# A hybrid decoder layer on one core: recurrent projections token-major, and every instruction issued from a recorded list

## The chip, the core and the metric

The kernel runs on one core of a Trainium2 chip. TensorE (PE) multiplies matrices into the accumulation memory (PSUM); VectorE (DVE), ScalarE (ACT) and GpSimd (POOL) work on arrays; SyncE (SP) issues transfers (DMAs) between the core's memory (SBUF) and the chip's main memory. Each engine executes its own instruction list in order and waits on semaphores where an instruction needs what another engine or a transfer makes. The metric is the device time of one execution in microseconds (us).

## The reference

One layer, 256 tokens, width 1024, float32:

```python
h = rmsnorm(x, norm1_g)
u = h @ w_in                       # columns: x_rnn | g_rnn | q | k | v | gates, 1024 each (gates 2048)
xa = causal_dwconv(x_rnn, conv_w, conv_b)                  # 4 taps over the tokens
ya = rg_lru(xa, w_r, b_r, w_i, b_i, lam) * gelu(g_rnn)     # block-diagonal gates, then a scan over tokens
yb = attention(rmsnorm(q), rmsnorm(k), v)                  # 8 heads of 128; one block of 256, so causal attention
merged = sigmoid(g_A) * (ya @ w_proj_rnn) + sigmoid(g_B) * (yb @ w_proj_attn)
x = x + merged @ w_out
h = rmsnorm(x, norm2_g)
x = x + (gelu(causal_dwconv(h @ w_up)) * (h @ w_gate)) @ w_down      # D_FF 2816
```

## The kernel before

**Products.** Each float32 operand is split into a rounded high part and a low remainder, and each product is three matmuls: high by high, low by high, high by low (lines 293 to 295, `mm3`). A product can be laid out in two ways. Feature-major (`fm_mm`, line 297): a 128x128 piece of the weight is held in the array and the 256 tokens stream past, so that the result has channels on the partitions; one matmul is 256 columns. Token-major (`tm_mm`, line 524): 128 tokens are held and 512 weight columns stream past, so that the result has tokens on the partitions; one matmul is 512 columns. In the kernel before, x_rnn (`rx`) and g_rnn (`rg`) are feature-major; k, q, v, the gates (`ga`, `gb`), both merge projections (`pr`, `pa`) and nearly all of up and gate (`up`, `gt`) are token-major.

**Units and chunks.** `UNITS` gives the order of PE's units: rx0 to rx3, rg0 to rg3, k0 to k3, ri0 (the block-diagonal r and i gates), q0, q1, ri1, ga, q, v and so on, then the merge, w_out, and the feed-forward part. Each unit consumes one chunk of weights, 1 MB. `load_next` (line 256) issues its DMA on SP into one of three `raw` buffers; `split_part` (line 274) makes `hi` on ACT (line 275; four buffers) and `lo` on DVE (line 276; three buffers). The table `AFTER` says at which quarter of which unit the other work is recorded, for instance "k1.3": "s11 conv2 decay" records the split of chunk 11, a convolution and the decay constants. Within that order, the scheduler of the tile framework places the instructions on ACT, DVE, POOL and SP; only the splits of the first stage are in written order on ACT and DVE (line 399).

**First stage.** Four chunks (rx) come in pieces of one, one, two, two and two k-tiles, each piece one DMA per chunk: rows of 1 KB for the first two pieces, then 2 KB, beside pieces of the transposed input `xT`. `xgh` and `xgl` are the input times norm1_g, split (lines 403 and 406). PE first runs `WARM` = 9 matmuls on a constant (line 342).

**Norm and layout.** The factor 1/rms of a token is computed while PE already multiplies (`norm1_stats`, line 416). For feature-major results it must lie along the free axis: `norm1_bcast` (line 425) spreads it with two matmuls, and DVE multiplies it in while it empties PSUM (line 470 for rx, line 724 for rg). For token-major results it is a scalar per partition, and ACT applies it.

**Turns.** q, k, up and gate are wanted feature-major and come out token-major. `turn` (line 314) turns them: DVE transposes 32x32 blocks (lines 321 and 323), four DMAs write the half (512 KB) to main memory, and a fifth, placed by its own item of `AFTER`, reads it back.

**Second norm.** `norm2_t` (line 785) transposes x on PE and makes the split input of the feed-forward part with four ACT and four DVE instructions of 128x128 in each of four calls (lines 794 and 795).

**Recurrence.** `rx_conv` (line 472) convolves along tokens, `ri_split` and `ri` make the gates, `lru_a` to `lru_d` the scan, `ya_mul` (line 660) multiplies by gelu(g_rnn).

Of the kernel before, what the change touches and what calls it, by code (L numbers as in the profile page):

```python
# [8 lines left out]
F32 = mybir.dt.float32  # L9
# [3 lines left out]
OP = mybir.AluOpType  # L13
# [17 lines left out]
HALVES, SMALLS, WARM, RAWS = 23, 10, 9, 3  # L31
# [6 lines left out]
    "rx0.0": "stats s4",  # L38
    "rg0.2": "bcast",
    "rg1.0": "evac3",  # L40
    "rg1.2": "s5",
    "rg1.3": "s6",
    "rg2.0": "evac0",
    "rg2.1": "evac2",
    "rg3.1": "evac1 conv0",
    "rg3.3": "s7",
    "k0.0": "s8 s9",
    "k1.0": "gelu1",
    "k1.1": "s10",
    "k1.3": "s11 conv2 decay",  # L50
    "k2.0": "krs0 s12 conv1 conv3",
    "k2.1": "split0 split1",
    "k2.2": "s13",
    "k2.3": "s14",
    "k3.2": "ks0",
    "ri0.0": "s15",
    "ri0.2": "krs1",
    "q1.3": "ks1 rk1",
    "ri1.2": "rk0",
    "ri1.3": "s16",  # L60
    "ga0.2": "rq0",
    "ga1.0": "qrs0",
    "ga1.2": "s17",
    "q2.0": "s18",
    "q3.0": "s19",
    "q3.2": "Tq0 Tk0",
    "v0.3": "s20",
    "v1.0": "Tk1",
    "v1.1": "la0",
    "v1.2": "S3 s21",  # L70
    "ga2.1": "rq1 S0 S1 Tq1 S2",
    "ga2.2": "s22 P3",
    "ga2.3": "s23",
    "ga3.0": "s24 s25 lb0 la1",
    "ga3.1": "lb1 lc1 ld1",
    "ga3.2": "P1",
    "v2.0": "s26",
    "v2.1": "qrs1 P0 P2",
    "v2.2": "gelu0 s27",
    "v2.3": "S4 s28",  # L80
    "v3.1": "S7",
    "v3.3": "S6",
    "gb0.0": "s29",
    "gb0.1": "lc0",
    "gb1.0": "S5",
    "gb1.1": "P4 s30",
    "gb1.2": "O3",
    "gb1.3": "O1",
    "gb2.0": "s31",
    "gb2.1": "O2",  # L90
    "gb2.3": "ld0",
    "gb3.0": "ya1 ya0",
    "gb3.1": "s32 P5 ys0",
    "gb3.2": "O4",
    "gb3.3": "sb0 s33",
    "pr0.1": "P7",
    "pr0.3": "s34 ys1",
    "pr1.1": "s35",
    "pr1.2": "sa1 sa0",
    "pr1.3": "O5 P6",  # L100
    "pr2.1": "s36",
    "pr2.3": "O7",
    "pr3.0": "O0",
    "pr3.1": "s37 O6",
    "pr3.3": "sb1",
    "pa2.2": "m0",
    "pa3.2": "s38",
    "pa3.3": "s39",
    "wo.1": "m1",
# [3 lines left out]
    "wo.12": "n00 s41",  # L113
    "wo.13": "n10",
    "up00.0": "s42 n01",
    "up00.2": "s43 n11",
    "gt00.3": "s44",
    "up01.1": "s45",
    "up01.3": "s46",
    "gt01.2": "s47",  # L120
    "up10.0": "ur0 s48",
    "up10.1": "s49",
    "up10.2": "bcast2",
    "up11.0": "s50",
    "up11.1": "s51",
    "up11.2": "fu0",
    "gt10.0": "s52",
    "gt10.1": "gr0",
    "up20.2": "s53",
    "up20.3": "ur1",  # L130
    "up21.0": "fg0",
    "up21.3": "s54 fu1",
    "gt20.2": "s55",
    "gt20.3": "gr1",
    "dn1.3": "s56 fg1",
    "up30.3": "s57 s58",
    "up31.0": "s59",
    "up31.2": "gr2",
    "up31.3": "s60 ur2",
    "gt31.0": "ur3",  # L140
    "gt31.1": "s61",
    "gt31.3": "fu2 s62",
    "dn2.0": "fu3 s63",
    "dn2.1": "fg2",
    "dn2.2": "s64",
    "dn3.0": "s65",
    "up40.0": "gr3",
    "gt40.0": "s66",
    "gt41.1": "s67",
    "gt41.2": "s68 fg3",  # L150
    "gt41.3": "ur4",
    "dn4.0": "s69",
    "dn4.1": "gr4",
    "dn5.1": "fu4",
    "dn5.2": "s70",
    "dn6.2": "s71",
    "dn7.0": "fg4",
    "last.3": "s72",
    "dn8.1": "s73",
    "dn9.3": "s74",  # L160
}


@with_exitstack
def trunk_layer(ctx: ExitStack, tc: tile.TileContext, xT, x, vec, win_fm, win_tm, wri, wpr, wpa,
                wout, wup, wgate, wdown, out):
    nc = tc.nc
    PSUM = bass.MemoryType.PSUM
    const = ctx.enter_context(tc.tile_pool(name="const", bufs=1))
    wp = ctx.enter_context(tc.tile_pool(name="wp", bufs=RAWS))  # L170
    halfp = ctx.enter_context(tc.tile_pool(name="halfp", bufs=HALVES))
    work = ctx.enter_context(tc.tile_pool(name="work", bufs=2))
    dram = ctx.enter_context(tc.tile_pool(name="dram", bufs=4, space=bass.MemoryType.DRAM))
    psA = ctx.enter_context(tc.tile_pool(name="psA", bufs=4, space=PSUM))
    psB = ctx.enter_context(tc.tile_pool(name="psB", bufs=4, space=PSUM))
# [30 lines left out]
    class Wide:  # L206


        def __init__(self, name, dt=F32):
            self.h = [half(f"{name}{i}", dt) for i in range(2)]  # L210

        def __getitem__(self, at):
            s = at[1]
            i = s.start // 1024
            assert (s.stop - 1) // 1024 == i
            return self.h[i][:, s.start - i * 1024:s.stop - i * 1024]

# [12 lines left out]
    source = {"rx": lambda c: win_fm[c], "rg": lambda c: win_fm[4 + c], "ri": lambda c: wri[c],  # L230
# [100 lines left out]
    tok32 = lambda a, t: a.rearrange("p (c t i b) -> p t c i b", t=2, i=4, b=32)[:, t]  # L331
# [3 lines left out]
    pv = const.tile([P, V_N], F32, name="pv")  # L335
    nc.scalar.dma_start(pv, vec)
# [8 lines left out]
    pieces = [(0, 1), (1, 2), (2, 4), (4, 6), (6, 8)]  # L345
    START = 4
    for i in range(START):
        if i < 2:
            raw[i] = wp.tile([P, 2048], F32, tag="raw", name=f"raw{i}")
            split_tiles()  # L350
        else:
            raw[i], hi[i], lo[i] = Wide(f"raw{i}"), Wide(f"hi{i}", F32R), Wide(f"lo{i}", F32R)
    ptr["load"] = ptr["split"] = START
    xs = const.tile([P, 2, D], F32, name="xs")
    for a, b in pieces:
        nc.sync.dma_start(kt(xTs.half(a // 4))[:, a % 4:a % 4 + b - a, :], xT[:, a:b, :])
        for i in range(START):
            s = slice(a * 256, b * 256)
            (nc.scalar if b <= 2 and i >= 2 else nc.sync).dma_start(raw[i][:, s], stream[i][:, s])
        if a == 0:  # L360
            nc.scalar.preload_act_table(AF.Exp)
        if a == 4:
            for t in range(2):
                nc.sync.dma_start(xs[:, t, :], x[t * P:(t + 1) * P, :])
# [3 lines left out]
    make_identity(nc, ident)  # L368
# [30 lines left out]
    with tc.manual_schedule(engines={mybir.EngineType.Activation, mybir.EngineType.DVE}):  # L399
        for a, b in pieces:  # L400
            for k in range(a, b):
                g = pv[:, V_G1 + k:V_G1 + k + 1]
                nc.scalar.activation(xgh[k], xTs[k], AF.Copy, scale=g)  # L403
                if a == 0:
                    split_part(0, slice(a * 256, b * 256), True)
                nc.vector.scalar_tensor_tensor(xgl[k], xTs[k], g, f(xgh[k]), op0=OP.mult, op1=OP.subtract)
            for i in range(a == 0, START):
                split_part(i, slice(a * 256, b * 256))

    rbc = const.tile([P, S], F32, name="rbc")  # L410
    rs1 = const.tile([P, 2], F32, name="rs1")
    dg = const.tile([P, 2, P], F32, name="dg")

    squared = []

    def norm1_stats():
        ss = const.tile([P, 2], F32, name="ss1")
        sq = half("sq1")
        for t in range(2):
            squared.append(nc.scalar.activation(sq, xs[:, t, :], AF.Square, accum_out=ss[:, t:t + 1]).ins)  # L420
        rsqrt(ss, rs1, 1.0 / D, 2)
        for t in range(2):
            nc.vector.tensor_scalar(dg[:, t, :], ident, rs1[:, t:t + 1], None, op0=OP.mult)

    def norm1_bcast():

        ps = bank("rbcp")
        for t in range(2):
            nc.tensor.matmul(ps[:, t * P:(t + 1) * P], ones, dg[:, t, :], start=True, stop=True)
        nc.scalar.copy(rbc, ps[:, :S])  # L430
# [4 lines left out]
    def make_decay():  # L435
# [9 lines left out]
        with tc.issue_after(squared[-1]):  # L445
            nc.scalar.activation(w[:, 1, :], w[:, 0, :], AF.Exp, scale=-1.0)
# [22 lines left out]
    def rx_evac(c, ps):  # L469
        nc.vector.tensor_mul(xr.pair(c), ps, rbc[:, None, :].to_broadcast([P, 2, S]))  # L470
# [66 lines left out]
    nc.vector.scalar_tensor_tensor(gqk, pv[:, V_QG:V_QG + 1], SC, pv[:, V_KG:V_KG + 1], op0=OP.mult, op1=OP.mult)  # L537
# [116 lines left out]
    rbc2 = rbc[:, None, :].to_broadcast([P, 2, S])  # L654
    open_ps, rx_ps = {}, {}
# [4 lines left out]
    def ya_mul(h):  # L660
        nc.vector.tensor_mul(gr.half(h), gr.half(h), it.half(h))

    def ya_split(h):
        split2(yah.half(h), yal.half(h), gr.half(h))
# [33 lines left out]
    evac = {"v": v_evac, "pr": pr_evac, "pa": pa_evac, "ga": lambda g, ps: gate_evac(sga, g, ps),  # L698
            "gb": lambda g, ps: gate_evac(sgb, g, ps)}

    def run_unit(kind, c):

        i = chunk[kind, c]
        if kind == "rx":

            for n in range(START):
                rx_ps[n] = kt(psA.tile([P, 512], F32, tag="A", name=f"rx{n}"))
            for k in range(KT):
                for n in range(START):
                    fm_mm(rx_ps[n], n, xgh, xgl, (k,), True)  # L710
            yield
            return
# [5 lines left out]
        elif kind == "rg":  # L718
            ps = fm_ps(f"{kind}{c}")
            for j in range(2):  # L720
                for h in range(2):
                    fm_mm(ps, i, xgh, xgl, range(4 * h, 4 * h + 4), js=(j,))
                    if j and h:
                        nc.vector.tensor_mul(gr.pair(c), ps, rbc2)
                    yield
        else:
            g, kh = c // 2, c % 2
            if not kh:
                open_ps[kind] = [bank(f"pa{g}{t}") if kind == "pa" else
                                 psA.tile([P, 512], F32, tag="A", name=f"{kind}{g}{t}") for t in range(2)]  # L730
# [9 lines left out]
    for n in range(4):  # L740
        item[f"evac{n}"] = lambda n=n: rx_evac(n, rx_ps[n])
        item[f"conv{n}"] = lambda n=n: rx_conv(n)
# [293 lines left out]
```

## Time and profile before

| | |
|---|---|
| time, median of 3 runs | 440.4 us (440.0 to 441.07) |
| profiled execution, its own time | 440.18 us |
| span of the profiled execution | 438.4 us |
| PE busy | 431.3 us, 98% |
| DVE busy | 325.1 us, 74% |
| ACT busy | 248.5 us, 57% |
| POOL busy | 45.8 us, 10% |
| moved by DMA | 95.89 MB, mean 219 GB/s |

The span runs from the first to the last instruction of the profiled execution. A busy share is an average over stages. Matmuls are pipelined: the duration of one matmul in the profile is longer than the distance from its start to the start of the next, so what a stream of matmuls costs is read from starts. PE's records count an operation on plain float32 operands (warm-up, transposes) twice.

### The profile page before, as it was taken

The numbers are of one execution on the slowest core, as the hardware profiler recorded it, in microseconds if no ns is written. First come the engines' busy times: TensorE is split into PE (matmuls) and PEld (weight loads), VectorE is DVE, ScalarE is ACT, GpSimd is POOL, SyncE is SP. The second block draws the span as 40 slices with busy tenths as digits, with TensorE's granted clock in tenths as the row PEclk, the third lists the DMA queues.
The fourth block names the chain that finished last, engine by engine and source line by source line (L and its number), as shares of the span: only waits on it lengthen the run. The fifth ranks groups of instructions, "written<-read, shape, count | busy, mean of one in ns | idle before, by whom it ended". The sixth has DMA issues, their size and how long they took to land.

```text
span 438.4 us, 5841 instructions
## 1 busy us (share of the span) xinstructions
PE 431.3 (98%) x2224; PEld 368.4 (84%) x2224; DVE 325.1 (74%) x448; ACT 248.5 (57%) x294; POOL 45.8 (10%) x99
## 2 busy tenths in 40 slices
PE   8999999999899999999999999999999999999996
PEld 8999988887788888888888888888888888888985
DVE  4689869768789999765576796576776779965943
ACT  4596748682888999944232373345437257352910
POOL 2038306424240000000000000000000000000000
PEclk9999999999999999999999999999999999999999
DMA  7987652857877754554553555877995494897202
GB/s 218 387 310 256 229 193 62 240 227 233 301 253 238 230 184 151 183 171 171 191 193 96 193 191 155 280 284 275 321 309 187 148 395 190 293 340 288 86 1 96
DMA packets 30268, 95.89 MB, mean 219 GB/s; under 512 B 2848, under 2 KB 12448, under 8 KB 26144
## 3 DMA queue, kind: packets, MB, share of 16 engines
q1 hardware_dynamic: 29520, 94.91, 62.0%
q10 hardware_dynamic: 720, 0.61, 0.6%
q8 instruction: 17, 0.28, 0.3%
q14 instruction: 11, 0.09, 0.1%
HBM read 87.12 MB, written 8.39 MB: 218 GB/s over the span
## 4 chain that ended last, share of the span: by engine, by line
PE 87%; DVE 5%; POOL 3%; DMA 2%; issue 1%; ACT 1%; SPq 0%; DVEq 0%
PE acc L293 4%; PE acc L294 4%; PE acc L295 4%; PE up L293 4%; PE up L294 4%; PE gt L293 4%; PE gt L294 4%; PE up L295 4%; PE gt L295 4%; POOL rsq L388 2%; DMA raw<-in_win_fm 2%; PE rg L295 2%; PE rg L294 2%; PE rg L293 2%; PE gb L293 2%; PE v L294 2%
## 5 line engine op out<-in xcount | busy, mean ns | idle before, releaser
L276 DVE TENSOR_TENSOR lo<-raw,hi 128x2048 fp32r<-128x2048 f32 (+3 forms) x92 | 170.9, 1868 | 40.1 <-ACT hi L275 8.5
L275 ACT CAST hi<-raw 128x2048 fp32r<-128x2048 f32 (+3 forms) x88 | 137.6, 1576 | 90.7 <-PE pa L295 16.0
L294 PE MATMUL up<-lo,h2h 128*128 128x512 f32 x80 | 31.2, 391 | 0.0
L294 PE MATMUL gt<-lo,h2h 128*128 128x512 f32 x80 | 31.1, 389 | 0.0
L294 PE MATMUL acc<-lo,fah 128*128 128x512 f32 x80 | 31.1, 389 | 0.0
L293 PE MATMUL acc<-hi,fah 128*128 128x512 f32 x80 | 31.1, 389 | 0.0
L295 PE MATMUL up<-hi,h2l 128*128 128x512 f32 x80 | 31.0, 389 | 0.0
L295 PE MATMUL gt<-hi,h2l 128*128 128x512 f32 x80 | 31.0, 389 | 0.0
L293 PE MATMUL up<-hi,h2h 128*128 128x512 f32 x80 | 30.9, 392 | 0.0
L293 PE MATMUL gt<-hi,h2h 128*128 128x512 f32 x80 | 30.8, 389 | 0.0
L295 PE MATMUL acc<-hi,fal 128*128 128x512 f32 x80 | 30.5, 389 | 0.0
L853 ACT ACTIVATE fc<-fu,pv 128x256 f32<-128x256 f32 x20 | 10.4, 590 | 19.8 <-DVE fu L865 19.8
L293 PE MATMUL rx<-xgh,hi 128*128 128x256 f32 x64 | 18.3, 288 | 0.8 <-ACT xgh L403 0.8
L295 PE MATMUL rx<-xgh,lo 128*128 128x256 f32 x64 | 18.2, 284 | 0.2 <-DVE lo L276 0.2
L293 PE MATMUL rg<-xgh,hi 128*128 128x256 f32 x64 | 18.2, 284 | 0.0
L294 PE MATMUL rx<-xgl,hi 128*128 128x256 f32 x64 | 18.2, 284 | 0.0
L295 PE MATMUL rg<-xgh,lo 128*128 128x256 f32 x64 | 18.1, 283 | 0.0
L294 PE MATMUL rg<-xgl,hi 128*128 128x256 f32 x64 | 18.1, 283 | 0.0
L293 PEld LDWEIGHTS up<-hi,h2h 128*128 128x128 f32 x80 | 15.0, 188 | 3.3 <-ACT h2h L794 0.2
L293 PEld LDWEIGHTS gt<-hi,h2h 128*128 128x128 f32 x80 | 15.0, 188 | 3.2
L295 PEld LDWEIGHTS gt<-hi,h2l 128*128 128x128 f32 x80 | 15.0, 188 | 3.2
L295 PEld LDWEIGHTS acc<-hi,fal 128*128 128x128 f32 x80 | 15.0, 188 | 3.1
(251 smaller groups left out, 1078.5 us busy)
## 6 DMA issues: line engine op xcount, KB each, us to landing
raw<-in_win_tm SPq DMA_DIRECT2D x12, 1024.0 KB, 5.2
raw<-in_win_fm SPq DMA_DIRECT2D x11, 1024.0 KB, 5.7
raw<-in_wup SPq DMA_DIRECT2D x11, 1024.0 KB, 5.7
raw<-in_wgate SPq DMA_DIRECT2D x11, 1024.0 KB, 5.7
raw<-in_wdown SPq DMA_DIRECT2D x11, 1024.0 KB, 6.0
raw<-in_wpr SPq DMA_DIRECT2D x4, 1024.0 KB, 5.0
raw<-in_wpa SPq DMA_DIRECT2D x4, 1024.0 KB, 4.9
raw<-in_wout SPq DMA_DIRECT2D x4, 1024.0 KB, 4.8
```

Of the source, the lines that this page charges most:

```text
L275: (nc.vector.tensor_copy if on_dve else nc.scalar.copy)(hi[i][:, s], raw[i][:, s])
L276: nc.vector.tensor_sub(lo[i][:, s], raw[i][:, s], f(hi[i][:, s]))
L293: nc.tensor.matmul(o, ah, bh, start=start, stop=False, skip_group_check=skip)
L294: nc.tensor.matmul(o, ah, bl, start=False, stop=False, skip_group_check=skip)
L295: nc.tensor.matmul(o, al, bh, start=False, stop=stop, skip_group_check=skip)
L388: nc.gpsimd.tensor_tensor(z, y, y, op=OP.mult)
L853: nc.scalar.activation(c, u, AF.Identity, scale=w(2), bias=pv[:, V_FB + m:V_FB + m + 1])
```

## The change

1. `rx` and `rg` become token-major. `run_unit` multiplies rx with 128 tokens held and 512 columns streaming, k-tile by k-tile, into four PSUM tiles of the `psA` pool; rg takes the general token-major path with four banks of `psB`. `norm1_bcast`, its two matmuls and the copy after them are gone.
2. The results are emptied by ACT with the token's factor as scalar (`scaled`: four copies of 128x512 for rx, four for rg) and turned with `turn`, two halves each: per half one transpose of 128x1024 on DVE, four DMAs out, one back. For x, ACT then reorders the blocks with two copies per half (`rx_order`). For g_rnn, gelu works on the blocks as they come back and `ya_mul` reads them in block order, two instructions per half instead of one; the product is written to `it`.
3. The first stage is cut otherwise: four pieces of two k-tiles; each DMA takes two chunks with rows of 2 KB; only the first is cut in two. The norm weights come in a small DMA of their own (`g1`); all other vectors come after the rx chunks, and x after two further chunks. `WARM` is 11.
4. `norm2_t` makes the split input with one multiplication, one copy and one subtraction over all four k-tiles.
5. All operations are recorded (`Later`), PE's in one list and the others in another, and issued in the order of the list `ORDER` under a manual schedule for all engines. `Pool` gives a recorded tile its buffer when it is issued: the one whose last use lies furthest back. `AFTER` is new in most entries.
6. Two small POOL instructions replace the DVE instruction that makes `gqk`.

By the built instruction lists, PE goes from 2211 to 2031 matmuls: `rx` from 192 of 256 columns to 84 of 512 and 24 of 256, `rg` from 192 of 256 to 96 of 512, minus two for the spread, plus two for the warm-up. ACT loads its function tables 14 times instead of 11. SP issues 185 DMAs instead of 173 and ACT 1 instead of 5: 20 new ones for the four turns, fewer in the first stage.

```diff
-HALVES, SMALLS, WARM, RAWS = 23, 10, 9, 3
+HALVES, SMALLS, WARM, RAWS = 23, 10, 11, 3
...
+class Later:
...
+    def issue(self, order):
...
+        for self.now, (engine, name, a, k) in enumerate(ops):
+            getattr(engine, name)(*map(real, a), **{n: real(v) for n, v in k.items()})
...
+    load_x(0, 2)
+    load_w(0, 0, one)
+    nc.scalar.preload_act_table(AF.Exp)
+    load_w(0, 0, two_)
+    load_w(0, 1)
+    for a in range(1, 4):
+        load_x(2 * a, 2 * a + 2)
+        for c in range(2):
+            load_w(a, c)
...
-    def rx_evac(c, ps):
-        nc.vector.tensor_mul(xr.pair(c), ps, rbc[:, None, :].to_broadcast([P, 2, S]))
+    def scaled(name, ps):
+
+        r = half(name)
+        for t in range(2):
+            nc.scalar.activation(r[:, t * 512:(t + 1) * 512], ps[t], AF.Copy, scale=rs1[:, t:t + 1])
+        return r
...
+    def rx_evac(g):
+        turned_x[g] = half(f"xd{g}")
+        turn(f"xm{g}", turned_x[g], scaled(f"xs{g}", rx_ps[g]), f"rx{g}")
+
+    def rx_order(g):
+        for t in range(2):
+            nc.scalar.copy(plain(xr.half(g), t), blocks(turned_x[g], t))
...
+    def rg_evac(g):
+        turn(f"gm{g}", gr.half(g), scaled(f"gs{g}", rg_ps[g]), f"rgr{g}")
...
     def ya_mul(h):
-        nc.vector.tensor_mul(gr.half(h), gr.half(h), it.half(h))
+
+        for t in range(2):
+            nc.vector.tensor_mul(plain(it.half(h), t), plain(it.half(h), t), blocks(gr.half(h), t))
...
+            for a in range(KT // 2):
+                for g in range(2):
+
+                    for cs in (slice(0, 1), slice(1, 2)) if (a, g) == (0, 0) else (slice(0, 2),):
+                        for kk in range(2):
+                            k = 2 * a + kk
+                            h, l = shi[a, g][:, cs, kk], slo[a, g][:, cs, kk]
+                            for n, (x, w) in enumerate(((xgh, h), (xgl, h), (xgh, l))):
+                                for t in range(2):
+                                    nc.tensor.matmul(rx_ps[g][t].rearrange("p (c n) -> p c n", c=2)[:, cs],
+                                                     x[k][:, t * P:(t + 1) * P], w, start=k == n == cs.start == 0,
+                                                     stop=k == KT - 1 and n == 2, skip_group_check=True)
...
-        for k4 in range(4):
-            k = 4 * hf + k4
-            g = pv[:, V_G2 + k:V_G2 + k + 1]
-            nc.scalar.activation(h2h[k][:, ts], ps[:, k4, :], AF.Copy, scale=g)
-            nc.vector.scalar_tensor_tensor(h2l[k][:, ts], ps[:, k4, :], g, f(h2h[k][:, ts]),
-                                           op0=OP.mult, op1=OP.subtract)
+        g = pv[:, V_G2 + 4 * hf:V_G2 + 4 * hf + 4, None].to_broadcast([P, 4, P])
+        m = small(f"h2{t}{hf}", 512).rearrange("p (k t) -> p k t", k=4)
+        nc.vector.tensor_mul(m, ps, g)
+        split2(kt(h2h.half(hf))[:, :, ts], kt(h2l.half(hf))[:, :, ts], m)
...
+
+    with tc.manual_schedule():
+        nc.issue(ORDER)
```

More of the change, by code (lines that the diff above doesn't have):

```diff
@@ L6 @@
 from concourse._compat import with_exitstack
-from concourse.masks import make_identity
 F32 = mybir.dt.float32
@@ L204, in pair @@
             return kt(self.half(c // 2))[:, 2 * (c % 2):2 * (c % 2) + 2, :]
[L206 to L216, printed above, removed]
     stream = []
@@ L398, in trunk_layer, with split_x, split_w @@
     xgh, xgl = Act("xgh", F32R), Act("xgl", F32R)
[L399 to L410, printed above, removed]
+    def split_x(k):
+        g = g1[:, k:k + 1]
+        nc.scalar.activation(xgh[k], xTs[k], AF.Copy, scale=g)
+        return lambda: nc.vector.scalar_tensor_tensor(xgl[k], xTs[k], g, f(xgh[k]), op0=OP.mult, op1=OP.subtract)
+    def split_w(a, c, js=slice(0, 2), ks=slice(0, 2), e=nc.scalar.copy):
+        r, h, l = sraw[a, c][:, js, ks], shi[a, c][:, js, ks], slo[a, c][:, js, ks]
+        e(h, r)
+        return lambda: nc.vector.tensor_sub(l, r, f(h))
+    x = split_x(0)
+    w = split_w(0, 0, one, one, nc.vector.tensor_copy)
+    x()
+    w()
+    w = split_w(0, 0, one, two_, nc.vector.tensor_copy)
+    x = split_x(1)
+    x()
+    w()
+    split_w(0, 0, two_)()
+    split_w(0, 1)()
+    for a in range(1, 4):
+        for k in (2 * a, 2 * a + 1):
+            split_x(k)()
+        for c in range(2):
+            split_w(a, c)()
     rs1 = const.tile([P, 2], F32, name="rs1")
     dg = const.tile([P, 2, P], F32, name="dg")
-    squared = []
     def norm1_stats():
@@ L419, in norm1_stats @@
         for t in range(2):
-            squared.append(nc.scalar.activation(sq, xs[:, t, :], AF.Square, accum_out=ss[:, t:t + 1]).ins)
+            nc.scalar.activation(sq, xs[:, t, :], AF.Square, accum_out=ss[:, t:t + 1])
         rsqrt(ss, rs1, 1.0 / D, 2)
[L422 to L430, printed above, removed]
     cdec = const.tile([P, KT], F32, name="cdec")
@@ L717, in run_unit @@
                 yield
[L718 to L725, printed above, removed]
         else:
```

345 lines of the change are left out of this document (206 added, 139 removed), and 38 rows, old and new, of the table ORDER.

## The prediction, made before the result was known

> **What bounds the kernel now.** The page first (busy time, then shares of the chain that ended last), then PE's waits over the whole span.
>
> ```profile
> span 438.4 us, 5841 instructions
> PE 431.3 (98%) x2224; PEld 368.4 (84%) x2224; DVE 325.1 (74%) x448; ACT 248.5 (57%) x294; POOL 45.8 (10%) x99
> PE 87%; DVE 5%; POOL 3%; DMA 2%; issue 1%; ACT 1%; SPq 0%; DVEq 0%
> ```
>
> ```profile
> PE v L293 <- ACT hi L275: 0.9, 1, 0.9
> PE rx L293 <- ACT xgh L403: 0.8, 1, 0.8
> ```
>
> PE is the bound: busy 98%, 87% of the chain, and no wait of a microsecond once it multiplies data. So two things can move the time: what PE's stream costs from start to start, and the few places where it stops. Both are read from starts in the order of time, since a busy share hides a short stop under the modelled end of the matmul before.
>
> ```profile
> 5.42 0.69 PE L293 MATMUL rx<-xgh,hi 128*128 128x256 f32 x2 [0.76 <-ACT xgh L403]
> ...
> 29.52 0.28 PE L293 MATMUL rg<-xgh,hi 128*128 128x256 f32 x1
> ...
> 33.73 0.28 PE L295 MATMUL rg<-xgh,lo 128*128 128x256 f32 x1
> 33.84 0.61 PE L429 MATMUL rbcp<-dg,ones 128*128 128x128 f32 x4
> 34.21 0.36 PE L293 MATMUL rg<-xgh,hi 128*128 128x256 f32 x1
> ...
> 53.01 0.40 PE L293 MATMUL k<-hi,xgh 128*128 128x512 f32 x1
> ...
> 74.79 0.28 PE L293 MATMUL ri<-xah,hi 128*128 128x256 f32 x1
> ```
>
> Start to start, rg takes 53.01 - 29.52 = 23.49 us. The spread (rbcp) puts 0.48 us between two rg starts instead of 0.12, so it costs 0.37. That leaves 23.12 us for 192 matmuls of 256 columns: 0.1204 us each. The k units take 74.79 - 53.01 = 21.78 us for 96 of 512 columns: 0.2269 each. So a column costs 0.470 ns in the short form and 0.443 ns in the long one. The 0.28 and 0.40 us durations overlap and must not be multiplied by the counts: that would promise some 30 us.
>
> **The change part by part.**
>
> *PE's stream.* Columns stay the same; only the form changes. rx: before 192 x 0.1204 = 23.12; after 84 x 0.2269 + 24 x 0.1204 = 21.95; gain 1.17. rg: 23.12 to 96 x 0.2269 = 21.78; gain 1.34. The spread: gain 0.37. Sum 2.88 us, all on the path. [...]
>
> *First stage.* rx takes 29.52 - 5.42 = 24.10 us, 0.98 more than its stream, lost in small waits.
>
> ```profile
> 4.48 0.32 DVE L275 CAST hi<-raw 128x256 fp32r<-128x256 f32 x1 [0.31 <-DMA raw<-in_win_fm]
> 4.83 0.42 DVE L276 TENSOR_TENSOR lo<-raw,hi 128x256 fp32r<-128x256 f32 x1
> 4.86 0.51 ACT L403 ACTIVATE xgh<-xT,pv 128x256 fp32r<-128x256 f32 x1 [1.46 <-DMA raw<-in_win_fm]
> 5.40 0.48 DVE L406 SCALAR_TENSOR_TENSOR xgl<-xT,pv,xgh 128x256 fp32r<-128x256 f32 x1
> ```
>
> After, DVE must do cast, xgl and lo for two k-tiles ahead of PE's first 12 short matmuls: 2 x (0.32 + 0.48 + 0.42) = 2.44 us against 12 x 0.1204 = 1.44. If the first weights land at 4.48 as now, DVE ends at 6.92, the last two matmuls at 7.16, as if the stream had begun at 7.16 - 1.44 = 5.72. Now it begins in effect at 5.42 + 0.98 = 6.40, so the gain is 0.7. But the first transfers are 256 KB instead of 128 KB.
>
> ```profile
> raw<-in_win_fm SPq DMA_DIRECT2D x12, 256.0 KB, 6.0
> raw<-in_win_fm SPq DMA_DIRECT2D x4, 128.0 KB, 3.5
> 10.00:20.00 10.00, 9.78 (x80) 9.41 (x79) 7.38 (x13) 6.65 (x13) 0.00 (x0) 1.00 1.02 376
> ```
>
> From 128 KB to 256 KB landing goes from 3.5 to 6.0 us, but the longer one under full load (the third row: DMA share 1.02, 376 GB/s); 256 KB more at 376 GB/s is 0.7 us. Bounds: 0 to 2.5 us later, a gain of 0.7 to a loss of 1.8. I take 0.5 later, nearest to the rate row: gain 0.2. Later pieces are covered: per two k-tiles DVE makes two lo of 1024 (four times the 0.42 row at most, 3.4) and two xgl (1.0), 4.4 us at most, and PE takes 24 x 0.2269 = 5.45. The two more warm-up matmuls lie under DVE's 2.44 us: PE could not use an earlier start.
>
> *Emptying and turning.* These rows price it:
>
> ```profile
> L323 DVE STREAM_TRANSPOSE kd<-kr 128x1024 f32<-128x1024 f32 x2 | 2.4, 1218 | 0.0
> L470 DVE TENSOR_TENSOR xr<-rx,rbc 128x512 f32<-128x512 f32 x4 | 2.6, 683 | 0.0
> L677 ACT ACTIVATE sga<-ga,rs 128x512 f32<-128x512 f32 x4 | 2.6, 688 | 3.7 <-PE ga L295 3.7
> L511 ACT ACT_TABLE_LOAD x2 | 2.6, 1283 | 0.0
> L794 ACT ACTIVATE h2h<-h2T,pv 128x128 fp32r<-128x128 f32 x16 | 5.3, 365 | 3.6 <-DVE h2l L795 3.1 <-PE h2T L790 0.3
> km<-kd SPq DMA_DIRECT2D x8, 128.0 KB, 2.5
> kd<-km SPq DMA_DIRECT2D x2, 512.0 KB, 5.8
> DMA packets 4581, 9.43 MB, mean 314 GB/s; under 512 B 498, under 2 KB 1906, under 8 KB 4338
> ```
>
> DVE loses 8 multiplications at 0.68 (5.5 us) and gains 4 transposes at 1.22 (4.9). ACT gains 8 scaled copies at 0.69 (5.5), 4 reordering copies of the same size (nearest row the scaled copy: 0.69 each, 2.8; twice that if the block order halves their speed) and 3 table loads at 1.28 (3.9); in the second norm it loses 16 x 0.365 (5.8) for 4 copies at about 0.69 (2.8). So ACT gains some 9 us of 438, two hundredths of the span, and DVE nothing.
>
> None of this is on PE's path while its covers hold. For x the edit adds two scaled copies 1.4, a transpose 1.2, writes 2.5, a read 5.8 and two reordering copies 1.4, together 12.3 us, between rx's end and the convolution. The cover is rg and k, 21.8 us each, which stand between rx and ri; ri waits for the chain if it is gone, and then up to 12.3 us show. g_rnn is wanted only by the merge, after all of attention: hidden. PSUM: k needs rx's four tiles, and the copies that free them need the token's factor, and that needs x, which lands behind two more chunks: 5.2 + 2.1 + 1.05 = 8.4 MB, by 27 us at 314 GB/s (the last row, the mean of the first 30 us). The rows' squares and the factor add a few us; k starts near 50 us. POOL's two instructions for gqk wait for vectors that now come late, but their reader comes only behind the first turn of k: nothing. ya_mul's two halves cost what its one instruction cost.
>
> *Second norm.* Three instructions of about 0.69 replace four pairs that pass back and forth (ACT waited 3.1 us for DVE there, the row above); PE had no stop there to lose, so nothing. If the longer first step (a whole multiplication and copy before the first k-tile is ready, about 1.4 us against 0.37) came onto the path, it would cost 1 us per call at two calls.
>
> *The order.* After rx and the first norm, PE stops at these places:
>
> ```profile
> 96.91 0.39 PE L293 MATMUL ga<-hi,xgh 128*128 128x512 f32 x1
> 97.40 0.50 PE L294 MATMUL ga<-lo,xgh 128*128 128x512 f32 x1
> ...
> 102.77 0.39 PE L293 MATMUL q<-hi,xgh 128*128 128x512 f32 x1
> 103.18 0.50 PE L294 MATMUL q<-lo,xgh 128*128 128x512 f32 x1
> ...
> 115.58 0.22 PE L294 MATMUL s<-kTl,qTh 128*128 128x128 f32 x1
> 116.70 0.73 PE L293 MATMUL v<-hi,xgh 128*128 128x512 f32 x2 [0.90 <-ACT hi L275]
> ...
> 118.20 0.28 PE L295 MATMUL s<-kTh,qTl 128*128 128x256 f32 x1
> 119.03 0.51 PE L294 MATMUL v<-lo,xgh 128*128 128x512 f32 x1 [0.55 <-DVE lo L276]
> ```
>
> Beyond the normal distance: 0.26, 0.18, about 1.0 and 0.71, with some 0.1 for each restart 2.6 us. At each, the split of a chunk came after other work on ACT or DVE. A list over all engines can put the split first, so the gain has bounds 0 and 2.6; new stops, which the trace of before cannot show, have the same source. I take half, 1.3, as the balance: the middle, since no row is nearer to one end.
>
> *Sum.* 2.88 + 0.2 + 1.3 = 4.4 us off the profiled execution's 440.18 (span 438.4 and 1.8 around it, unchanged; the tail after the last matmul is untouched). That execution lies 0.2 under the median of 440.4, so on medians 440.4 - 4.4 = **436.0 us**.
>
> **The rivals.**
>
> *All stops go and the start gains too.* 440.4 - 2.88 - 0.7 - 2.6 = 434.2. For it: DVE and ACT have slack on average. Against: the stretch below.
>
> *ScalarE becomes the bound in attention.*
>
> ```profile
> 140.00:160.00 20.00, 20.00 (x101) 16.82 (x100) 19.00 (x30) 19.94 (x26) 0.00 (x0) 1.00 0.62 209
> ```
>
> In these 20 us (busy time of PE, weight load, DVE, ACT in this order) ACT is busy for 19.94. The extra table loads fall here, between the softmaxes: 3 x 1.283 = 3.85 us if all of it reaches PE, so 439.8: no change. Against: the splits run ahead of PE by a chunk, and PE had no stop here.
>
> *SP's queue holds up the weights: slower.*
>
> ```profile
> SPq L265 <- DVE lo L276: 106.4, 26, 10.8
> SPq L328 <- DMA upm<-fupd: 4.5, 1, 4.5
> 100.00:120.00 20.00, 18.53 (x91) 15.21 (x91) 16.02 (x17) 11.04 (x11) 7.47 (x13) 1.00 0.86 289
> raw<-in_win_tm SPq DMA_DIRECT2D x12, 1024.0 KB, 5.2
> ```
>
> Each new turn's read waits on SP for its four writes, up to 4.5 us, and the loads behind it wait too. In the issue order the turns of q, k and g_rnn crowd together: between five loads stand eight half-turns, 5 x 1.05 + 8 x 0.52 = 9.4 MB in 5 x 5.45 = 27 us, 346 GB/s; 289 at a share of 0.86 gives 336 when full. A load has the time of three chunks, 16.3 us, less cast and lo (about 4.2) and landing (5.2): 6.9 us of slack, and PE stops once hold and longer landing exceed it. Four holds of 2.5 us beyond it are 10: 446. Against: SP mostly waits for a free buffer (26 times, 106 us), so loads go out as soon as they may.
>
> [...]
>
> **How the numbers follow.** Main case 0.52 (its own range 434.8 to 438.6), all stops gone 0.15, ScalarE 0.13, SP 0.17, gap rule 0.03. Faster by over 0.3% (1.3 us, about what a measurement can tell from no change) is main, first and last: 0.70; within 0.13; slower 0.17. The range 433.5 to 441.5 takes in all but SP's case and an edge of the first: it holds about 0.8.
>
> **What would show it.** Right: rg starts 0.227 apart, from first rg to first k 21.8 us; first rx to first rg 22 to 23 us; no spread; rx's emptying on ACT far ahead of k. For the order: PE's waits between 95 and 120 us near nothing. Wrong: PE waiting for casts behind table loads near 150 us, weight loads landing late behind a turn's read near 85 to 115 us, or a first rx after 7 us.

## The result, and the profile after

The changed kernel takes 434.9 us (median of 4 runs, 434.67 to 435.03); the kernel before took 440.57 us beside it (440.0 to 441.07). The ratio is 0.9871, with a 95% interval of 0.9854 to 0.9888: 1.3% faster, some 5.7 us. The prediction was 436.0 us, with a range of 433.5 to 441.5.

The page of the changed kernel, for its profiled execution of 435.01 us: the span, PE's busy time, and the shares of the chain that ended last. Nearly every instruction stands at line L296 now, since one loop issues them; groups are told apart by the tile.

```profile
span 433.2 us, 5466 instructions
PE 428.4 (99%) x2044; PEld 360.0 (83%) x2044; DVE 326.8 (75%) x426; ACT 256.9 (59%) x285; POOL 50.1 (12%) x101
PE 97%; DMA 1%; DVE 0%; SPq 0%; ACT 0%; issue 0%
```

PE was 87% of the chain and is 97% of it. PE's waits over the whole span (the sum, how many, the longest, in us):

```profile
PE warm L296 <- DVE ones L296: 1.0, 1, 1.0
PE rx L296 <- ACT his L296: 0.2, 1, 0.2
```

Once PE multiplies data, one wait is left, of 0.2 us. PE's instructions of the changed kernel in the order of time (start, duration) at the borders of the units:

```profile
5.75 0.68 PE L296 MATMUL rx<-his,xgh 128*128 128x256 f32 x2
...
28.93 0.39 PE L296 MATMUL rg<-hi,xgh 128*128 128x512 f32 x1
29.16 0.39 PE L296 MATMUL rg<-lo,xgh 128*128 128x512 f32 x1
...
50.70 0.39 PE L296 MATMUL k<-hi,xgh 128*128 128x512 f32 x1
...
72.45 0.28 PE L296 MATMUL ri<-xah,hi 128*128 128x256 f32 x1
...
429.47 0.28 PE L296 MATMUL end<-hi,fa 128*128 128x256 f32 x1
```

The same last row of the kernel before:

```profile
434.59 0.28 PE L295 MATMUL end<-hi,fa 128*128 128x256 f32 x1
```

PE ends 5.12 us earlier, and the two profiled executions differ by 5.17. Where it came from, by starts:

| part | before | after | gain |
|---|---|---|---|
| first rx starts at | 5.42 | 5.75 | -0.33 |
| first rx to first rg | 24.10 | 23.18 | 0.92 |
| first rg to first k | 23.49 | 21.77 | 1.72 |
| first k to first ri | 21.78 | 21.75 | 0.03 |
| first ri to last matmul | 359.80 | 357.02 | 2.78 |
| sum | | | 5.12 |

In the last part lie the three stops near 97, 103 and 115 to 119 us, 2.6 us in all before. None of them is left: the distances there are the stream's own (two starts of the gates in the changed kernel, where the kernel before had stopped at the same pair).

```profile
94.58 0.39 PE L296 MATMUL ga<-hi,xgh 128*128 128x512 f32 x1
94.80 0.39 PE L296 MATMUL ga<-lo,xgh 128*128 128x512 f32 x1
```

The two stretches that the rivals named, of the changed kernel (busy time of PE, weight load, DVE, ACT, POOL; then clock, DMA share, GB/s):

```profile
100.00:120.00 20.00, 20.00 (x90) 16.55 (x89) 18.74 (x19) 14.16 (x12) 14.28 (x23) 1.00 1.02 345
140.00:160.00 20.00, 20.00 (x99) 16.70 (x98) 17.79 (x34) 19.36 (x29) 0.00 (x0) 1.00 0.62 218
```

Between 100 and 120 us the DMAs are full (share 1.02 and 345 GB/s; 0.86 and 289 before), and PE does not stop. In attention ACT is busy for 19.36 us of 20, no more than before in the same stretch (19.94).

### The profile page after: what moved, and what is told of

Its sections match the earlier page's. It is cut to its first block, busy times and chain, and to the rows that moved or that the text cites. A ratio compares the mean times of both kernels' runs of the same rounds, so it can differ in the third digit from the quotient of the medians.

```text
span 433.2 us, 5466 instructions
## 1 busy us (share of the span) xinstructions
PE 428.4 (99%) x2044; PEld 360.0 (83%) x2044; DVE 326.8 (75%) x426; ACT 256.9 (59%) x285; POOL 50.1 (12%) x101
## 4 chain that ended last, share of the span: by engine, by line
PE 97%; DMA 1%; DVE 0%; SPq 0%; ACT 0%; issue 0%
PE acc L296 14%; PE up L296 13%; PE gt L296 13%; PE pr L296 5%; PE gb L296 5%; PE yo L296 5%; PE ga L296 5%; PE v L296 5%; PE pa L296 5%; PE q L296 5%; PE k L296 5%; PE rg L296 5%; PE rx L296 4%; DMA raws<-in_win_fm 1%; PE gtl L296 1%; PE upl L296 1%
## 5 line engine op out<-in xcount | busy, mean ns | idle before, releaser
L296 DVE TENSOR_TENSOR lo<-raw,hi 128x2048 fp32r<-128x2048 f32 (+1 forms) x72 | 160.0, 2224 | 27.2 <-issue 9.5
L296 ACT CAST hi<-raw 128x2048 fp32r<-128x2048 f32 (+1 forms) x69 | 128.4, 1863 | 87.0 <-PE up L296 11.5
L296 PE MATMUL up<-hi,h2h 128*128 128x512 f32 x80 | 31.4, 393 | 0.0
L296 PE MATMUL up<-hi,h2l 128*128 128x512 f32 x80 | 31.1, 389 | 0.0
L296 PE MATMUL acc<-hi,fah 128*128 128x512 f32 x80 | 31.1, 389 | 0.0
L296 PE MATMUL acc<-lo,fah 128*128 128x512 f32 x80 | 31.1, 389 | 0.0
L296 PE MATMUL gt<-hi,h2l 128*128 128x512 f32 x80 | 31.1, 389 | 0.0
L296 PE MATMUL gt<-hi,h2h 128*128 128x512 f32 x80 | 31.1, 389 | 0.0
L296 PE MATMUL gt<-lo,h2h 128*128 128x512 f32 x80 | 31.1, 389 | 0.0
L296 PE MATMUL acc<-hi,fal 128*128 128x512 f32 x80 | 31.1, 389 | 0.0
L296 PE MATMUL up<-lo,h2h 128*128 128x512 f32 x80 | 31.1, 389 | 0.0
L296 DVE SCALAR_TENSOR_TENSOR fc<-fu,pv,fc 128x255 f32<-128x255 f32 (+1 forms) x40 | 17.0, 475 | 2.0 <-ACT fc L296 1.9
L296 POOL TENSOR_TENSOR rsq<-rsq 128x8 f32<-128x8 f32 x32 | 17.1, 533 | 11.8 <-DVE rsq L296 9.6
L296 PEld LDWEIGHTS acc<-hi,fal 128*128 128x128 f32 x80 | 15.0, 188 | 3.2
L296 PEld LDWEIGHTS gt<-hi,h2h 128*128 128x128 f32 x80 | 15.0, 188 | 3.1
L296 PEld LDWEIGHTS up<-hi,h2l 128*128 128x128 f32 x80 | 15.0, 188 | 3.1
L296 PEld LDWEIGHTS acc<-hi,fah 128*128 128x128 f32 x80 | 15.0, 188 | 3.1
L296 PEld LDWEIGHTS gt<-lo,h2h 128*128 128x128 f32 x80 | 15.0, 188 | 3.1
L296 PEld LDWEIGHTS gt<-hi,h2l 128*128 128x128 f32 x80 | 15.0, 188 | 3.1
L296 PEld LDWEIGHTS up<-hi,h2h 128*128 128x128 f32 x80 | 15.0, 188 | 3.0
L296 PEld LDWEIGHTS acc<-lo,fah 128*128 128x128 f32 x80 | 15.0, 188 | 3.0
```

The source lines that it names most:

```text
L296: getattr(engine, name)(*map(real, a), **{n: real(v) for n, v in k.items()})
```

## The experiments

Each time stands beside runs of the kernel before on the same chip (440.2 to 440.8 us).

### rg alone, on the kernel before

rg token-major, emptied by ACT and turned, `ya_mul` in blocks; all else as before.

```diff
-    "k1.0": "gelu1",
+    "k1.0": "rgr0",
...
+            nc.scalar.activation(r[:, t * 512:(t + 1) * 512], rg_ps[g][t], AF.Copy, scale=rs1[:, t:t + 1])
+        turn(f"gm{g}", gr.half(g), r, f"rgr{g}")
```

> The kernel before with rg alone token-major, emptied by ACT and turned; rx, the spread of the norm and the scheduler as before. Theory A (price from the rows, 0.1204 and 0.2269 us a matmul): first rg to first k falls from 23.49 to 22.15 us, time 439.2. [...] Rival C: two more turns in the scheduler's order bring new stops: above 441.

Measured: 440.23 us, ratio 0.9996 (0.9985 to 1.0007). PE's starts in this kernel:

```profile
29.76 0.39 PE L293 MATMUL rg<-hi,xgh 128*128 128x512 f32 x1
30.47 0.50 PE L294 MATMUL rg<-lo,xgh 128*128 128x512 f32 x1 [0.32 <-DVE lo L276]
...
52.66 0.39 PE L293 MATMUL k<-hi,xgh 128*128 128x512 f32 x1
```

First rg to first k is 22.90 us, with the spread's 0.37 still in it and a new stop of 0.59 (0.48 at the second rg matmul, 0.11 behind it). Without these two, 21.94: the stream gains what the rows had said (21.78). But the other layout needs its whole first chunk sooner, and that stop takes half of the gain; the first rg starts 0.24 us later besides (29.76 against 29.52), so that k starts only 0.35 us earlier. The three stops stay (1.02 and 0.70 of them at v), so this layout of rg is not what removed them.

### The second norm alone, on the kernel before

```diff
-            nc.scalar.activation(h2h[k][:, ts], ps[:, k4, :], AF.Copy, scale=g)
-            nc.vector.scalar_tensor_tensor(h2l[k][:, ts], ps[:, k4, :], g, f(h2h[k][:, ts]),
-                                           op0=OP.mult, op1=OP.subtract)
+        nc.vector.tensor_mul(m, ps, g)
+        split2(kt(h2h.half(hf))[:, :, ts], kt(h2l.half(hf))[:, :, ts], m)
```

> The kernel before with the second norm's new form alone (one multiplication, one copy, one subtraction per call). Theory (the prediction's): PE had no stop there, nothing moves: 440.4 (440 to 440.9). Rival: the first k-tile of a call is ready 1 us later and PE stops for it at two calls: 442.5.

Measured: 440.73 us, ratio 1.0005 (0.9995 to 1.0015). Nothing, although ACT's work here fell from 16 x 365 ns to four copies of 622 ns.

### The layout without the list

The changed kernel without `Later`, `Pool` and `ORDER`: the framework's scheduler places the instructions, with the new `AFTER`; only the splits of the first stage keep a written order on ACT and DVE.

```diff
-    nc = Later(tc.nc)
+    nc = tc.nc
...
+    with tc.manual_schedule(engines={mybir.EngineType.Activation, mybir.EngineType.DVE}):
...
-    with tc.manual_schedule():
-        nc.issue(ORDER)
```

> The changed kernel without the recorded list: the framework's scheduler orders the instructions by the table AFTER, everything else (token-major rx and rg, turns, first stage, second norm) stays. Theory A (the prediction's split): PE's stream keeps its 2.9 us, the stops come back, some 2.6 us: 437.5 (436 to 438.5), PE stops near 90 to 125 us, first rg to first k still 21.8 us. Rival B: the list does nothing: 434.9, no stops. Rival C: the new turns need the list to stay out of the weights' way: 440 or more, with weight loads late.

Measured: 445.45 us, ratio 1.0122 (1.0098 to 1.0145): slower than before, and 10.5 us behind the changed kernel. PE's waits in it:

```profile
PE rx L882 <- ACT his L549: 3.5, 2, 1.9
PE k L417 <- DVE lo L399: 2.3, 1, 2.3
```

First rx to first rg is 28.46 us, 5.3 more than with the list; k and ri lose 4.2. In rx PE stops twice, for 2.0 and 1.8 us, and runs at half its clock behind the first stop (0.43 us between starts instead of 0.227, 1.7 us more; see the last section). The first stop is for a cast that waits for its load and starts at 9.53 us, where the list has it at 8.31. Ahead of the second one, ACT:

```profile
21.12 0.21 ACT L592 ACTIVATE decw<-decw 128x8 f32<-128x8 f32 x1 [6.17 <-POOL decw L588]
21.23 1.98 ACT L549 CAST his<-raws 128x1024 fp32r<-128x1024 f32 x2
```

ACT stands for 6.17 us at the decay constants, which wait for the vectors that now come late, and the casts that PE needs are behind them.

In k and ri SP looks like the cause. Its DMA issues in this kernel (start, time taken for the group):

```profile
33.01 3.46 SPq L388 DMA_DIRECT2D raw<-in_win_tm  x2
40.04 3.76 SPq L450 DMA_DIRECT2D xm<-xd  x8
```

Between 36.5 and 50.4 us no weights are asked for, since the writes of x's turn, which wait for DVE's transposes, stand first. With the list three loads go out there (at 36.85, 42.14 and 48.02). But it is not the late load that stops PE. The chunk at which it stops, the last of k, is asked for at 59.82 us and has landed at 65.46, and PE comes to it at 71.8. ACT's cast and DVE's low part of that chunk (the first of the two in each group):

```profile
70.89 2.85 ACT L398 CAST hi<-raw 128x2048 fp32r<-128x2048 f32 x2
74.96 3.42 DVE L399 TENSOR_TENSOR lo<-raw,hi 128x2048 fp32r<-128x2048 f32 x2
```

From 65.86 us on ACT works without a pause, but on the emptying of k and on the convolution, 5 us long, with the cast behind; the low part stands behind DVE's share of the convolution (twelve instructions, 4.8 us). So the layout alone costs 5 us, and the list is worth 10.5 in it; some 6 of these are lost by the order on ACT and DVE. The time is that of the expectation's third case; its reason, weights that come late behind the turns, is not what PE waited for.

The stops at 97 to 119 are gone here too, all but 0.29. That does not clear the list of them: the split of the second gate chunk starts 4.8 us later than in the kernel before (99.85 against 95.06), but PE begins the gates 6.7 us later (98.12 against 91.44). PE's earlier stops can have given the splits their lead.

### The splits forward, on the kernel before

```diff
+    "ga0.0": "s17",
...
-    "ga1.0": "qrs0",
-    "ga1.2": "s17",
-    "q2.0": "s18",
-    "q3.0": "s19",
+    "ga1.0": "s18 qrs0",
+    "q2.2": "s19",
+    "q3.0": "s20",
```

> The kernel before, with four entries of AFTER moved so that the splits of ga1, q2, q3 and v0 (and the loads that go with them) are recorded earlier, ahead of the emptying of q. Theory A: the three stops of before (2.6 us at 97, 103 and 115 to 119 us) come from other work standing ahead of the splits on ACT and DVE: stops there under 1 us, time 438.5. Rival B: they come from weights that land late behind the turns: stops stay near 2.6, time 440.5.

Measured: 446.21 us, ratio 1.0127 (1.0109 to 1.0145). The stops at 97 and 103 stay (0.23 and 0.13), and v is worse:

```profile
116.14 1.07 PE L295 MATMUL v<-hi,xgh 128*128 128x512 f32 x2 [1.88 <-ACT hi L277]
118.47 0.80 PE L296 MATMUL v<-lo,xgh 128*128 128x512 f32 x1 [1.26 <-DVE lo L278]
```

The weights of v are not late: they had landed at 110.0 us. Their cast starts at 114.20, since ACT, idle from 104.9 on, stands for 8.68 us at the squares of q, which wait for PE. Earlier entries in the table are not earlier splits: the scheduler weighs all work again.

### The new table alone, on the kernel before

`AFTER` of the changed kernel from q1 to the end, for the items that exist in both.

```diff
-    "ga1.2": "s17",
-    "q3.2": "Tq0 Tk0",
-    "v0.3": "s20",
-    "v1.1": "la0",
+    "ga1.1": "s17 Tk0",
+    "q3.2": "Tq0",
+    "v0.0": "s20",
+    "v1.1": "qrs0",
```

> The kernel before, with the changed kernel's table AFTER from q1 to the end, for the items that exist in both; rx, rg, the turns of q, k, the first stage and the framework's scheduler stay as before. Open is what removed the three stops near 97, 103 and 115 to 119 us (2.6 us): written issue alone did not, since the changed kernel without its list has them no more. If the table removes them, PE stops there for 0.5 us at most and the time is about 440.4 - 2.6 = 437.8. If the token-major layout does (ACT and DVE have other work in front of the splits there), they stay and the time is 440.4 within 0.4. If the framework's scheduler does with this table what it did with the splits moved forward, new stops of 1 to 2 us come in v and the time is 442 or more.

Measured: 445.16 us, ratio 1.009 (1.0066 to 1.0114). The third case of the expectation came in its time. v is better (0.19 instead of 1.73), but q stops for 2.7 us. PE, then DVE in this kernel:

```profile
104.32 0.39 PE L290 MATMUL q<-hi,xgh 128*128 128x512 f32 x1
107.24 0.50 PE L291 MATMUL q<-lo,xgh 128*128 128x512 f32 x1 [2.54 <-DVE lo L273]
```

```profile
102.49 1.22 DVE L495 TENSOR_TENSOR rt<-rt,cdec 128x1024 f32<-128x1024 f32 x1
...
103.77 1.22 DVE L502 TENSOR_TENSOR it<-it,xa 128x1024 f32<-128x1024 f32 x1
104.91 2.28 DVE L273 TENSOR_TENSOR lo<-raw,hi 128x2048 fp32r<-128x2048 f32 x1
```

Two multiplications of the recurrence, 1.2 us each, stand ahead of the split that PE needs at 104.5. This is the prediction's "the split of a chunk came after other work on ACT or DVE", in the plainest row of the study. The table without the list does not remove the stops; it moves them.

### Warm-up of 9

Two warm-up matmuls fewer, in the list too; its order is else the same.

```diff
-HALVES, SMALLS, WARM, RAWS = 23, 10, 11, 3
+HALVES, SMALLS, WARM, RAWS = 23, 10, 9, 3
```

> The changed kernel with 9 warm-up matmuls instead of 11. Theory A (the prediction's): the warm-up ends under DVE's first splits, nothing moves: 434.9 (434.5 to 435.3), rx takes 23.2 us from first rx to first rg. Rival B: the warm-up holds PE, first rx at 5.4 instead of 5.75 us, time 0.3 less. Rival C: the shorter warm-up leaves a pause and the granted clock falls: the first rx matmuls are spaced wider, time 0.5 to 2 more.

Measured: 434.37 us (434.25 to 435.14), ratio 0.9867 (0.9851 to 0.9882), not to be told from the changed kernel. The first rx starts at 5.29 instead of 5.75 and the first rg at 29.08 instead of 28.93: PE waits longer for the second chunk instead (0.69 us, 0.24 in the changed kernel).

### The second chunk's first transfer on ACT's queue

```diff
-    load_w(0, 1)
+    load_w(0, 1, e=nc.scalar)
```

> The changed kernel with one DMA of the first stage (the first piece of rx's second pair of chunks, 512 KB, which PE waits for at 8.8 us) issued from ACT instead of SP. Theory A: the first stage is limited by the rate at which one queue issues (4 DMAs in 1.9 us): the two stops of 0.40 and 0.45 us go, first rx to first rg 22.4 instead of 23.2 us, time 434.1. Rival B: it is limited by what the DMAs move (about 300 GB/s then): 434.9, or the first weights land later for it.

Measured: 435.73 us, ratio 0.989 (0.987 to 0.991). The wait for the second chunk goes, but the first chunk comes later:

```profile
6.81 0.47 PE L296 MATMUL rx<-his,xgh 128*128 128x256 f32 x2 [1.33 <-DVE his L296]
```

First rg is at 29.57 instead of 28.93. What the DMAs move from 1 to 10 us is nearly the same (293 GB/s, and 287 in the changed kernel), so the earlier issue took its time from the transfers beside it: here what the DMAs move is the limit, not when SP asks for it.

### Four casts twice

The casts of chunks 24, 26, 28 and 30 are issued twice, 7.5 us more on ACT in attention.

```diff
+TWICE = range(24, 32, 2)
...
+                if j in TWICE:
+                    nc.times[id(nc.ops[-2][2])] = 2
```

> The changed kernel with the ACT casts of chunks 24, 26, 28 and 30 (in attention, about 135 to 180 us) done twice: 4 x 1.9 = 7.5 us more on ACT where it is busy 19.4 and 19.6 of 20 us. Rival (ScalarE is the bound there): nearly all of it reaches PE, 440 to 442. Theory (the splits run ahead, and the work behind them can slide to the freer stretch from 180 us on): under 2 us, 435 to 437.

Measured: 441.53 us, ratio 1.003 (1.0015 to 1.0044), 6.6 us over the changed kernel. PE in this kernel:

```profile
167.86 0.77 PE L298 MATMUL gb<-hi,xgh 128*128 128x512 f32 x1 [5.50 <-DVE vl L298]
```

Of 7.5 us of added work 6.6 reach PE, so with the change ACT has about a microsecond to spare there. (The profiled execution took 443.69 us; twelve matmuls at half the clock, 0.43 us apart, follow its stop.)

### The new turns' DMAs twice: both, x alone, g_rnn alone

```diff
+            for _ in range(self.times.get(id(a), 1)):
...
+        twice = name[0] in "xg" and name[:2] != "gt"
```

For x alone the condition is `name[0] == "x"`, for g_rnn alone `name[0] == "g" and name[:2] != "gt"`.

> The changed kernel with every DMA of the four new turns (x and g_rnn: four writes and the read of each half) issued twice: 4.2 MB more and 20 more entries in SP's queue, the same data. Theory A (slack): a weight load has 6.9 us to spare and PE sees under 1 us: 435 to 436. Rival B (SP's queue and a full DMA bound PE, as the slower rival had it): the traffic of the stretch from 80 to 120 us is full already (share 1.02), 2.1 MB more there at 345 GB/s are 6 us, which PE waits for: 441 or more.

> The changed kernel with every DMA of the turns of x (four writes and a read per half) issued twice; the turns of g_rnn stay single. Doubling both cost 42.6 us. The x turns come before k, the g_rnn turns between them and k's weight loads. If SP's queue and the DMAs have a margin of some microseconds, as the prediction had it (6.9 us of slack per load), this alone costs nothing up to 2 us: 435 to 437. If the margin is nearly nil, the 2 x (0.5 + 0.5) MB more at 345 GB/s, 6 us, and the holds of the second reads reach PE in the k units: 441 to 452, with stops near 66 to 70 us and none near 137.

> The same with the turns of g_rnn twice and those of x single. With a margin of some microseconds: 435 to 437. With none: the load of k's later chunks comes late, and the time is 441 to 455; the stops of 6 to 7 us near 137 to 144 us, which the doubling of both had, then belong to these turns only if they show again here. If both halves alone cost less than 10 us together, the loss of 42.6 is one of a queue that overflows once, not a price per DMA.

Measured: both 477.49 us, ratio 1.0845 (1.0815 to 1.0874); x alone 455.44, 1.0313 (1.0278 to 1.0347); g_rnn alone 458.09, 1.039 (1.036 to 1.0419). Over the changed kernel that is 42.6, 20.5 and 23.2 us: the two add up. Both single ones cost more than their expectations' worst case. SP's queue in the kernel with x twice, its waits and its issues:

```profile
SPq L297 <- DMA xm<-xd: 19.2, 8, 4.8
...
SPq L297 <- DMA xd<-xm: 11.8, 2, 6.0
```

```profile
35.53 13.48 SPq L297 DMA_DIRECT2D xm<-xd  x8
49.05 0.43 SPq L297 DMA_DIRECT2D raw<-in_win_tm  x1
49.58 13.29 SPq L297 DMA_DIRECT2D xm<-xd  x8
62.97 0.38 SPq L297 DMA_DIRECT2D raw<-in_win_tm  x1
```

The edit did more than it was meant to. A second copy goes to the same place as the first, so SP waits for the first to land, eight times for the writes. It tests a held queue, not fuller transfers: from 35 to 63 us this kernel moves 147 GB/s, the changed one 280. The two loads go out at 49.05 and 62.97 instead of 36.85 and 42.14, 12.2 and 20.8 us late. The first is absorbed. The second stops PE for 3.6 us, and then comes a stop that no load explains (PE, then DVE):

```profile
66.85 0.39 PE L297 MATMUL k<-hi,xgl 128*128 128x512 f32 x1
70.64 0.80 PE L297 MATMUL k<-hi,xgh 128*128 128x512 f32 x1 [3.40 <-ACT hi L297]
78.66 0.80 PE L297 MATMUL k<-lo,xgh 128*128 128x512 f32 x1 [7.22 <-DVE lo L297]
```

```profile
74.93 1.47 DVE L297 SCALAR_TENSOR_TENSOR xa<-xr,pv,xa 128x255 f32<-128x255 f32 x3 [16.21 <-ACT xa L297]
76.32 2.29 DVE L297 TENSOR_TENSOR lo<-raw,hi 128x2048 fp32r<-128x2048 f32 x1
```

DVE stands for 16.21 us at the convolution, which waits for x's turn, and the split that PE needs is behind it. With g_rnn twice PE waits for ACT's copy of k behind its turn (5.8 us) and then for the softmax (8.0 in three stops).

So holds on SP come through at about two thirds (20.5 us of 31.0 for x; 23.2 of 38.4 for g_rnn, by the waits 22.3 for its writes and 16.1 for its reads), and by way of other engines' order as much as through late weights. These runs do not measure what full transfers alone would cost; that stays open.

## Why the prediction was right, and where it was not

**PE's stream: right.** rg starts are 0.227 us apart, and first rg to first k gained 1.72 us where 1.34 + 0.37 were predicted; 21.77 measured, 21.78 forecast. The rg-alone run shows the same on the kernel before (21.94 without its stop and the spread). Beyond the spread, rg's conversion gave 1.35 us (1.72 - 0.37) where 1.34 were reckoned. No run shows the gap rule to which the forecast gave a chance of 0.03: the starts are 0.120 us apart in the short form (first rg to first k before, without the spread) and 0.227 in the long one.

**First stage: too favourable by 0.8 us.** The prediction had the first rg at 28.15 us (24.10 - 1.17 - 0.2 after 5.42); it came at 28.93, since the start is 0.33 later and 1.2 us are lost in rx beyond its stream of 21.95. The first piece was sized about rightly. The first weights are cast at 5.22 us instead of 4.48, 0.74 later where 0.5 was taken, but DVE is done in less than the reckoned 2.44 us, and the first 12 matmuls end at 7.57, as if the stream had begun at 7.57 - 1.44 = 6.13; the forecast was 5.72 + 0.5 = 6.22. The step that failed is "Later pieces are covered". It set DVE's work against PE's and had no landing in it. DVE, PE and ACT in the changed kernel, and the landing of the first stage's transfers:

```profile
5.22 0.29 DVE L296 CAST his<-raws 128x256 fp32r<-128x256 f32 x1 [4.24 <-DMA raws<-in_win_fm]
...
7.57 0.40 PE L296 MATMUL rx<-his,xgh 128*128 128x256 f32 x2
...
8.31 1.05 ACT L296 CAST his<-raws 128x1024 fp32r<-128x1024 f32 x1 [1.83 <-DMA raws<-in_win_fm]
...
9.41 0.74 PE L296 MATMUL rx<-his,xgh 128*128 128x512 f32 x2 [0.24 <-ACT his L296]
```

```profile
raws<-in_win_fm SPq DMA_DIRECT2D x2, 256.0 KB, 4.1
```

The first 256 KB landed better than feared (4.1 us, not 6.0). But the cast of the second pair of chunks waits for the 512 KB behind them, which land at 8.28, 6.2 us after their issue, and PE starts its next matmul at 9.41, 0.40 us late. At 10.67 it waits another 0.22 for DVE's low part. With 0.11 for each restart (0.34 us to the next start instead of 0.23, as behind the stop of the rg-alone run) these are 0.84 us, the 0.8 that the forecast lacks. The bounds, +0.7 to -1.8, held it. That the two more warm-up matmuls cost nothing was right.

**Emptying and turning, second norm: right.** Neither shows on PE's path, and the second norm by itself gives 0. But the reckoning of the cover, 43.6 us for the x chain, left out that the chain's copies and convolution stand on ACT and DVE among the casts of k. Without the list that costs 4.2 us at k and ri, though ri does not wait for the chain itself.

**The order: right in its mechanism, half its size.** All three stops went: 2.78 us from ri to the end against 1.3 taken. In the trace the list does what the step said it could. DVE's split for the pair at 94.58 us (97 before) in the changed kernel, and in the kernel before (the splits run in the order of the chunks; this is the second chunk of the gates):

```profile
86.26 2.29 DVE L296 TENSOR_TENSOR lo<-raw,hi 128x2048 fp32r<-128x2048 f32 x1
```

```profile
93.92 1.22 DVE L505 TENSOR_TENSOR it<-it,xa 128x1024 f32<-128x1024 f32 x1
95.06 2.28 DVE L276 TENSOR_TENSOR lo<-raw,hi 128x2048 fp32r<-128x2048 f32 x1
```

It ends 6.2 us before PE needs it (88.55 against 94.80), where before it ended at 97.34, after PE had come. The table alone, the splits moved by hand and rg's layout each leave stops, or make new ones. That the list by itself would remove them on the old layout was not tried, so its share is argued and not shown. What the step missed is the larger part of what the list does: it was priced as a gain of 0 to 2.6 us on the old order, while the layout without it loses 5 us to the kernel before. New stops were named as having the same source, and got no price. That the forecast came within 1.1 us of 434.9 is in part luck: the order gave 1.5 us more than taken and the first stage 0.8 less.

**The rivals.** All stops going was given 0.15, with 434.2 us; that happened to the stops, but the start lost where it was to gain. ACT in attention: the three more table loads do fall there (nine between 147 and 189 us, where the kernel before has six between 149 and 178), ACT is busy for 52.4 us of the 60 from 140 to 200 instead of 51.1, and PE does not stop. The doubled casts show that 7.5 us more bring 6.6, so the case was near. SP's queue: the DMAs are full there as reckoned (346 GB/s, 345 measured), but the holds were not as reckoned. SP's only wait above 1 us for the writes of a turn of x, g_rnn, q or k is this one:

```profile
SPq L296 <- DMA qm<-qd: 2.8, 1, 2.8
```

The list puts other issues between a turn's writes and its read, so the four holds of 2.5 us beyond the slack did not exist. That such holds would have cost what the rival said is borne out in kind by the doubled turns. A hold by itself need not cost anything: for the writes of up's and gate's turns SP waits 27.0 us in all (6.0 before), and PE does not stop for it.

## What to carry to other kernels

A bound engine's time is read from starts, per form of instruction, and a change of form could then be forecast here to a few hundredths of a microsecond (21.78 us for rg, 21.77 measured). A new layout that adds copies and transfers should be priced together with the order of every engine's list: here the same layout was 5 us slower or 5.7 us faster than before, by order alone, and in the slower one casts and splits stood behind other work of ACT and DVE. A load that goes out late is not yet the cause of a stop; compare its landing with the start of its cast (65.46 and 70.89 us for the last chunk of k without the list). When an experiment doubles a transfer into the same place, it doubles a wait as well (SP stood for 19.2 us at x's writes); look at the queue's rows before reading it as bandwidth.

## What was not expected of the hardware

After some longer stops PE runs at half its clock, and that adds to the stop: in the kernel with x's DMAs twice, matmuls are 0.43 us apart instead of 0.227 behind the stops of 3.40 and 7.22 us (clock 0.50 from 70 to 83 us, 1.00 again from 84 on). Not the length of a stop alone decides. The kernel with g_rnn's DMAs twice has a stop of 1.86 us that ends at 150.29 and is followed by half the clock, and one of 2.63 that ends at 159.35 and is not. Four stretches of 3.41 us in it (busy time of PE, clock, DMA share, GB/s):

```profile
147.79:151.20 3.41, 1.55 (x8) 1.00 0.71 290
151.20:154.61 3.41, 3.41 (x10) 0.50 0.48 149
154.62:158.03 3.41, 2.10 (x9) 1.00 1.02 410
158.03:161.44 3.41, 2.09 (x13) 1.00 0.15 60
```

In this kernel the stretches at half the clock begin at 123.90, 140.96, 151.20 and 185.34 us, which is 5, 3 and 10 times 3.41 apart. By the distances of its matmuls (0.43 us, then 0.23 again) they end near 130.7, 144.4, 154.6 and 188.8, the first after twice 3.41 us and the others after 3.41. Counted in steps of 3.41 us from these starts, the stop of 1.86 us lies whole in one step, and the one of 2.63 us is cut into 1.31 and 1.32. In other kernels half the clock follows the first stop of rx without the list (1.89 us) and the one at v with the splits forward (1.88, clock 0.50 from 119 to 123 us); it does not follow the second stop of rx without the list (1.62), the one at k there (2.30), or the one at q with the table alone (2.54). That the place of a stop in these steps decides is the author's estimate from these few stops; no run was made to test it. In the layout without the list, the half clock behind the first stop of rx came while PE was always busy and cost it half of 3.41, 1.7 us (mean clock 0.94 in the first 30 us). So that stop of 2.0 us cost nearly twice its length.
